# A hybrid decoder layer on one core: queries and keys copied out of PSUM once, head 0's keys split in a spare pad, two blocks of the final sums placed where block B11 was

## The chip, the cores and the metric

The kernel runs on one core of a Trainium2 chip. The core has five engines with an instruction queue each: TensorE (PE) multiplies matrices into eight banks of PSUM, VectorE (DVE), ScalarE (ACT) and GpSimd (POOL) compute on SBUF, DVE and ACT also on PSUM, and SyncE (SP) starts DMA transfers. The metric is the device time of one execution in microseconds. Before the change three runs took 1165.88, 1164.83 and 1165.71 us, a median of 1165.71.

## The reference

One layer of a decoder trunk in float32: 1024 tokens, 1024 channels, 8 heads of 64.

```
h = rms_norm(x, norm1_g)
q, k, v, glu_a, glu_b = split(h @ w_in)              # 512 columns each
q, k = rms_norm(q per head), rms_norm(k per head)
attn: z = q k / 8, strictly causal; weights[t,s] = sigmoid(z[t,s]) * prod_{s<j<t} (1 - sigmoid(z[t,j]))
c = glu_a * sigmoid(glu_b); causal depthwise conv of width 31; silu(layer_norm(c))
x = x + concat([attn, c]) @ w_out
h = rms_norm(x, norm2_g)
gate, val = split(h @ w_up)                          # 2816 columns each
x = x + (silu(causal_depthwise_conv3(gate)) * val) @ w_down
```

## The kernel before, in words

**Products.** Every float32 operand is split into a high and a low part of the type fp32r, and a product is three matrix multiplications: high by high (L281), low by high (L282) and high by low (L283). PE carries them all.

**Stages.** The kernel runs through these stretches of the profiled span: the input norm and its transposes (0 to 25 us); the projections of the glu, the conv, v, k and q of heads 0 to 3 (called v0, k0, q0), v of heads 4 to 7, and queries and keys of heads 4 to 7 together (qk0 to qk7, one for each tile of 128 tokens) up to some 240 us; attention, heads 0 to 7 one after the other, up to 457 us; the attention half of the output projection (opa), the second norm and its transposes up to 522 us; the up projection up to 939 us; and the down projection.

**Attention.** For a head, its keys are split into high and low on POOL (L905, L908), transposed on PE (kT, L922) and copied back; its queries are doubled by a DMA, transposed (qT, L956) and split by ACT and DVE. Then the queries go in eight tiles (tb 0 to 7) of 128 tokens, each against all keys up to its own: scores z on PE (L993, L996, with a mask L995), a sigmoid of −z into a row called nb and one of z into a row called wt (ACT, L1005 and L1008), a running product along nb (the scan on DVE, L1023), nb times wt on POOL (L1026), transposes of wt on PE (wT, L1049), their split (rest, L1053 on ACT or DVE, and tl, L1059 on DVE), and the product with v (po, L1065 and L1066). In the tile names the first number is the head and the next the tile: z0_4_1 is head 0, tile 4, second 512 columns. Where one head's tiles leave PE free, products of other stages fill in: qk0 to qk3, then the conv half of the output projection (op).

**What sets the order.** Up to the end of the second norm the order on PE, ACT, DVE and POOL is fixed by a planner in the kernel (class `Plan`). Every step has a cost, a due time ("key"), steps that it follows, and tokens of what it occupies: "s", "z" and "o" are PSUM banks, "nb" the four rows for the sigmoids, which are first the padded tiles ("pad") of the conv. The planner takes the step with the earliest start, or, among those within PATIENCE ns of it, the one with the earliest key, and writes the instructions in that order; `in_order` pins it. QK_TO and CONV_TO bound the keys over which the fillers are spread, W_SHIFT shifts the loads of the output weights, LEAD_LOAD says how far ahead of their use weights are loaded. From the up projection on, the framework's scheduler sets the order, and tile pools decide when a buffer is free.

**Norms of queries and keys.** `project` (k0, q0) and the steps for qk4 to qk7 leave the products in an "o" bank. ACT squares the eight groups of 64 columns with a sum each (L483, L804), POOL makes the reciprocal roots (`rstd`, L273), and ACT scales eight times into SBUF (L487, L808). The bank is held until then.

**Up and down projection.** The up projection multiplies by Strassen's scheme in blocks: tiles called 11, 21, 22, S1 and so on of the normed input, with block B11 in the tile "hh0" of the pool hp. The down projection adds its products from PSUM into four blocks of sums, 11, 12, 21 and 22 (L1626 on DVE); each starts from x, loaded by SP (L1604). Blocks 11 and 21 lie in a pool `dn` that opens when hp is closed, 12 and 22 in buffers of the up projection.

Of the kernel before, what the change touches and what calls it, by code (L numbers as in the profile page):

```python
# [16 lines left out]
P = 128  # L17
# [14 lines left out]
LEAD_LOAD, LEAD_W = 14.0, 11.0  # L32
# [144 lines left out]
def kernel(  # L177
# [54 lines left out]
    const([P, 24], F32, "pad")  # L232

    ident = const([P, P], F32, "ident")
    make_identity(nc, ident)
    ident_b = const([P, P], BF16, "ident_b")
    nc.vector.tensor_copy(ident_b, ident)
    ident_r = const([P, P], F32R, "ident_r")
    nc.vector.tensor_copy(ident_r, ident)
# [46 lines left out]
    small = ctx.enter_context(tc.tile_pool(name="small", bufs=1))  # L286
    mix_ctx = ExitStack()
    mixp = mix_ctx.enter_context(tc.tile_pool(name="mixp", bufs=1, reuse_waits="tile"))
    attn_out = mixp.tile([P, ND // 2, S], F32, tag="attn_out", name="attn_out")
# [4 lines left out]
    for tag in ("v0", "k0", "q0", "k1", "q1", "v1"):  # L294
        tile_of = qkvp.tile([P, 2, D], F32, tag=tag, name=f"x_{tag}")
        if tag not in ("v0", "k0"):
            xs.append(tile_of)
# [3 lines left out]
    wp = in_ctx.enter_context(tc.tile_pool(name="wp", bufs=1, side="right", reuse_waits="tile"))  # L301
    hp = hp_ctx.enter_context(tc.tile_pool(name="hp", bufs=1, side="right", reuse_waits="tile"))
# [33 lines left out]
    for n in range(2):  # L336
        h_hi.append(hp.tile([P, ND, HS], F32R, tag=f"hh{n}", name=f"h_hi{n}"))
        h_lo.append(hp.tile([P, ND, HS], F32R, tag=f"hl{n}", name=f"h_lo{n}"))
# [9 lines left out]
                 "qd": 2, "squares": 1, "whl": 8, "pair": 2, "norm": 4, "xsum": 2, "cacc": 2, "term": 3, "ln": 4},  # L348
# [93 lines left out]

    def project(part, blk, ws, pairs, ats):

        done.setdefault((part, blk), [])
        for pair, at_ in zip(pairs, ats):
# [31 lines left out]
            def square(d=d, pair=pair, dst=dst, o=o):  # L478
                d["sq"], d["rs"] = [small.tile([P, 8], F32, tag=f"{tag}8_{o.index}", name=f"{tag}_{part}{blk}_{pair}") for tag in ("sq", "rs")]
                d["to"] = dst().rearrange("p t (h d) -> p (t h) d", d=DH)  # L480
                d["from"] = d["ps"].rearrange("p t (h d) -> p (t h) d", d=DH)
                for i in range(8):
                    nc.scalar.activation(d["to"][:, i, :], d["from"][:, i, :], AF.Square, accum_out=d["sq"][:, i:i + 1])  # L483

            def scale(d=d):
                for i in range(8):
                    nc.scalar.activation(d["to"][:, i, :], d["from"][:, i, :], AF.Copy, scale=d["rs"][:, i:i + 1])  # L487

            a = add("ACT", 3500, square, T(at_ + 6), [m])
            b = add("POOL", 2700, lambda d=d: rstd(d["rs"], d["sq"], 1.0 / DH), T(at_ + 6), [a])  # L490
            a = add("ACT", 1850, scale, T(at_ + 6), [b])
            o.users += [a]
            done[part, blk] += [a]
# [287 lines left out]
    def queries_keys_in(t, at_):  # L781
# [3 lines left out]
        for k in range(ND):  # L785
            def products(k=k):
                if k == 0:
                    d["ps"] = bank(o, [P, 512], f"qk{t}")
                for part in "qk":
                    if (part, 1) not in qkv:  # L790
                        qkv[part, 1] = qkvp.tile([P, NT, 256], F32, tag=f"{part}1", name=f"{part}1")
# [8 lines left out]
        def square():  # L800
            d["sq"], d["rs"] = [small.tile([P, 8], F32, tag=f"{tag}8_{o.index}", name=f"{tag}_qk{t}") for tag in ("sq", "rs")]
            d["to"] = [qkv["qk"[i // 4], 1][:, t, i % 4 * DH:(i % 4 + 1) * DH] for i in range(8)]
# [301 lines left out]
    def w_out_rows(k):  # L1104
        room = plan.token("whl")

        def load():
            if not wd:
                for part in ("hh0", "hl0"):
                    wd[part] = hp.tile([P, 4 * S], F32R, tag=part, name=f"w_{part}")  # L1110
# [553 lines left out]
```

## Time and profile before

| what | value |
|---|---|
| median of three runs | 1165.71 us |
| profiled execution, its own time | 1162.9 us |
| its span | 1161.1 us |
| mean granted clock of TensorE | 0.987 |
| instructions | 16180 |
| transfers | 116.50 MB, 100 GB/s on average |

The page's span runs from the first to the last recorded instruction; the execution's own time is 1.8 us longer. In the windows, a row gives the window, its length, and then for each engine the busy time and, in brackets, the number of instructions: PE, its weight loads, DVE, ACT, POOL; after them the granted clock (1.00 is full speed), the share in which DMA engines were busy, and GB/s. In the table of waits a row gives the engine and line that waited, the engine, tile and line that released it, and the total, the number and the longest of the waits. In the timeline a row gives start, duration, engine, line, operation, output and input, and in square brackets the idle time before it with its releaser. Matmuls are pipelined, so their durations overlap; what one costs is the distance of the starts.

### The profile page before, as it was taken

How to read it: one execution, taken by the hardware profiler on the slowest of the kernel's cores; microseconds unless marked ns; L12 is line 12 of the kernel's file. 1: busy time of each engine (PE TensorE's matmuls, PEld its weight loads, DVE VectorE, ACT ScalarE, POOL GpSimd, SP SyncE). 2: the span in 40 equal slices, each digit the busy share in tenths (PEclk: the TensorE clock that was granted, in tenths of full speed). 3: DMA queues.
4: the chain of work that ended last, by engine and by line, in shares of the span. 5: the costliest groups of instructions: out<-in, count | busy, mean ns of one | idle time of the engine just before them, and what ended most of it. 6: DMA issues, size and time to landing. Idle time of an engine off the chain costs nothing.

```text
span 1161.1 us, 16180 instructions
## 1 busy us (share of the span) xinstructions
PE 1118.5 (96%) x5734; PEld 936.9 (81%) x5734; DVE 909.5 (78%) x1199; ACT 640.3 (55%) x1335; POOL 603.2 (52%) x505
## 2 busy tenths in 40 slices
PE   6999999989999997979999999999999989999998
PEld 5888899767788886868888888888888867888886
DVE  5399995549998888889887777777677679887895
ACT  6255576586987885554434333434333466766680
POOL 6077965486666652545522332233313167877880
PEclk8999999999999998989999999999999999999999
DMA  8011103122743114432332222222222461134303
GB/s 276 19 56 55 55 2 91 47 102 95 232 126 110 55 39 153 154 127 65 118 109 71 93 73 91 73 91 73 91 86 79 133 247 70 77 145 146 130 16 145
DMA packets 108638, 116.50 MB, mean 100 GB/s; under 512 B 20782, under 2 KB 88590, under 8 KB 108558
## 3 DMA queue, kind: packets, MB, share of 16 engines
q1 hardware_dynamic: 108414, 114.95, 30.0%
q8 instruction: 45, 0.74, 0.3%
q10 hardware_dynamic: 144, 0.52, 0.1%
q14 instruction: 35, 0.29, 0.1%
HBM read 82.95 MB, written 28.31 MB: 96 GB/s over the span
## 4 chain that ended last, share of the span: by engine, by line
PE 84%; DVE 6%; POOL 4%; ACT 3%; issue 2%; DMA 1%; SPq 0%; POOLq 0%; DVEq 0%; ACTq 0%
PE dn L1623 16%; PE u_S L281 7%; PE u_S L282 7%; PE u_S L283 7%; PE u L282 5%; PE u L281 5%; PE u L283 5%; PE wT L1049 2%; POOL attn_out L602 2%; PE po L1066 2%; PE v L281 1%; PE po L1065 1%; PE v L282 1%; PE v L283 1%; PE z L996 1%
## 5 line engine op out<-in xcount | busy, mean ns | idle before, releaser
L1623 PE MATMUL dn<-wd,wd 128*128 128x512 f32 x924 | 212.4, 390 | 5.3 <-DVE c L1626 2.7
L1623 PEld LDWEIGHTS dn<-wd,wd 128*128 128x128 f32 x924 | 172.6, 188 | 44.9 <-DVE c L1626 4.8
L1626 DVE TENSOR_TENSOR c<-dn,c 128x512 f32<-128x512 f32 x144 | 95.2, 683 | 24.1 <-PE dn L1623 22.8
L602 POOL TENSOR_TENSOR attn_out<-attn_out 128x512 f32<-128x512 f32 x60 | 83.3, 1389 | 54.2 <-ACT attn_out L599 50.4
L1532 ACT CAST wd<-rawd 128x512 fp32r<-128x512 f32 x154 | 87.0, 618 | 42.1 <-PE dn L1623 15.8
L1026 POOL TENSOR_TENSOR wt<-wt,nb 128x128 f32<-128x128 f32 (+3 forms) x64 | 78.2, 1228 | 56.6 <-DVE nb L1023 34.1
L282 PE MATMUL u_S<-bT,aS 128*128 128x512 f32 x264 | 102.7, 389 | 0.0
L283 PE MATMUL u_S<-bT,aS 128*128 128x512 f32 x264 | 102.7, 389 | 0.0
L281 PE MATMUL u_S<-bT,aS 128*128 128x512 f32 x264 | 102.4, 389 | 0.0
L277 ACT CAST aS<-rawu 128x512 fp32r<-128x512 f32 x63 | 39.0, 621 | 94.8 <-PE u_S L283 70.6
L1023 DVE TENSOR_TENSOR_SCAN nb<-nb,one 128x128 f32<-128x128 f32 (+3 forms) x64 | 85.3, 1344 | 6.8 <-ACT nb L1005 6.6
L1533 DVE TENSOR_TENSOR wd<-whole,wd 128x512 fp32r<-128x512 f32 x110 | 73.7, 683 | 10.7 <-ACT wd L1532 8.4
L1392 POOL TENSOR_TENSOR s<-rawu 128x512 f32<-128x512 f32 x21 | 29.9, 1426 | 99.5 <-DMA rawu<-in_w_up_dram 89.3
L1531 ACT COPY whole<-rawd 128x512 f32<-128x512 f32 x110 | 63.0, 584 | 29.7 <-DMA rawd<-in_w_down_dram 15.7
L1398 POOL TENSOR_TENSOR rawu<-rawu 128x512 f32<-128x512 f32 x21 | 29.0, 1381 | 82.3 <-DVE a L278 82.3
L282 PE MATMUL u<-b,a 128*128 128x512 f32 x176 | 70.0, 398 | 0.0
L281 PE MATMUL u<-b,a 128*128 128x512 f32 x176 | 69.9, 397 | 0.0
L283 PE MATMUL u<-b,a 128*128 128x512 f32 x176 | 69.2, 393 | 0.0
L277 ACT CAST a<-rawu 128x512 fp32r<-128x512 f32 x63 | 39.0, 621 | 51.5 <-PE u_S L283 34.7
L1487 DVE SCALAR_TENSOR_TENSOR y<-gv,cols_a,y 128x1023 f32<-128x1023 f32 (+1 forms) x44 | 58.6, 1333 | 8.3 <-ACT y L1485 8.2
L1533 POOL TENSOR_TENSOR wd<-rawd,wd 128x512 fp32r<-128x512 f32 x44 | 57.5, 1324 | 11.6 <-ACT wd L1532 9.7
L278 DVE TENSOR_TENSOR a<-rawu,a 128x512 fp32r<-128x512 f32 x63 | 47.0, 748 | 15.8 <-ACT a L277 15.8
(286 smaller groups left out, 3363.7 us busy)
## 6 DMA issues: line engine op xcount, KB each, us to landing
rawu<-in_w_up_dram SPq DMA_DIRECT2D x44, 512.0 KB
act_d<-y SPq DMA_DIRECT2D x22, 512.0 KB
rawd<-act_d SPq DMA_DIRECT2D x22, 512.0 KB
rawd<-in_w_down_dram SPq DMA_DIRECT2D x22, 512.0 KB
rawo<-in_w_out_dram SPq DMA_DIRECT2D x8, 512.0 KB
m<-conv_d SPq DMA_DIRECT2D x16, 256.0 KB
xt<-in_x_dram SPq DMA_DIRECT2D x8, 512.0 KB
x_part<-xt SPq DMA_DIRECT2D x8, 512.0 KB
```

What stands on the lines that cost most here:

```text
L277: nc.scalar.copy(hi, src)
L281: nc.tensor.matmul(ps, a_hi, b_hi, start=first, stop=False)
L282: nc.tensor.matmul(ps, a_hi, b_lo, start=False, stop=False)
L283: nc.tensor.matmul(ps, a_lo, b_hi, start=False, stop=last)
L602: last = add("POOL", 1310, lambda e=e: nc.gpsimd.tensor_tensor(d["c"], d["c"], e["t"], op=ALU.add), key(m, 16), [x, last])
L1023: nc.vector.tensor_tensor_scan(rev, rev, one.to_broadcast([P, w]), 1.0, op0=ALU.mult, op1=ALU.bypass)
L1026: nc.gpsimd.tensor_tensor(d["wt"][:, :w], d["wt"][:, :w], d["nb"][:, o + 1:S + 1], op=ALU.mult)
L1531: nc.scalar.copy(whole, src)
L1532: nc.scalar.copy(t[:, 0], src)
L1533: lo_engine.tensor_tensor(t[:, 1], whole, f32(t[:, 0]), op=ALU.subtract)
L1623: nc.tensor.matmul(ps, a[:, tok], b, start=first and m == 0, stop=last and m == 2, skip_group_check=True)
L1626: nc.vector.tensor_tensor(sums[c][s], ps, sums[c][s], op=ALU.add)
```

## The change

Six things, all in one edit (lines with "after" are those of the changed kernel):

1. `normalized()` (L447 to L470 after): one copy of the bank into SBUF, by ACT or DVE as the planner finds, and the "o" token is given back behind it. The squares are then taken from SBUF, all eight into one small tile `junk`, the scales in place. k0, q0 and qk4 to qk7 use it, twelve in all. For that, q and k of heads 4 to 7 become one tile, qk1.
2. Head 0's keys are split into a spare conv pad (`first_keys`, an "nb" token) instead of the tile "keys", which lies where the second half of the normed input was; so the split does not wait for the last use of that input (`second_used`), but the transposes and copies behind it do. The split's key is EARLY = 4 before the head instead of 2.6.
3. The first tile of the normed input, h_hi[0], later a part of the output weights and then block B11, lies in a pool of its own, hp0, that lives until the end. Sums 11 and 21 of the down projection are one tile c_1 in its place.
4. Constants: LEAD_LOAD 14 to 17, PATIENCE 50 to 200, QK_TO 6 to 7, W_SHIFT 0 to 0.5.
5. The identity is built in attn_out and only its fp32r copy is kept.
6. The constant pad shrinks from 24 to 8 columns.

The diff, cut to its core:

```diff
-LEAD_LOAD, LEAD_W = 14.0, 11.0
+LEAD_LOAD, LEAD_W = 17.0, 11.0
-HORIZON, PATIENCE = 3.0, 50
+HORIZON, PATIENCE = 3.0, 200
-QK_FROM, QK_TO = -3.0, 6.0
+QK_FROM, QK_TO = -3.0, 7.0
+EARLY = 4.0
-W_SHIFT = 0.0
+W_SHIFT = 0.5
...
+    made = attn_out[:, 1, :P]
+    make_identity(nc, made)
...
+    ident = f32(ident_r)
...
+    junk = const([P, DH], F32, "junk")
...
+    hp0 = in_ctx.enter_context(tc.tile_pool(name="hp0", bufs=1, side="right", reuse_waits="tile"))
...
-        h_hi.append(hp.tile([P, ND, HS], F32R, tag=f"hh{n}", name=f"h_hi{n}"))
+        h_hi.append((hp if n else hp0).tile([P, ND, HS], F32R, tag=f"hh{n}", name=f"h_hi{n}"))
...
+    def normalized(name, d, o, m, to, at_):
+        r = plan.token("rs8")
+        def out_of(eng):
+            (nc.scalar.copy if eng == "ACT" else nc.vector.tensor_copy)(to(), ...)
+        def square():
+            d["sq"], d["rs"] = [small.tile([P, 8], F32, tag=f"{tag}8_{r.index}", name=f"{tag}_{name}") for tag in ("sq", "rs")]
+            for i in range(8):
+                nc.scalar.activation(junk, to()[:, i * DH:(i + 1) * DH], AF.Square, accum_out=d["sq"][:, i:i + 1])
+        def scale():
+            for i in range(8):
+                group = to()[:, i * DH:(i + 1) * DH]
+                nc.scalar.activation(group, group, AF.Copy, scale=d["rs"][:, i:i + 1])
+        c = add({"ACT": 600, "DVE": 690}, out_of, T(at_), [m])
+        o.users += [c]
+        a = add("ACT", 3500, square, T(at_), [c], [r])
+        b = add("POOL", 2700, lambda: rstd(d["rs"], d["sq"], 1.0 / DH), T(at_), [a])
+        a = add("ACT", 1850, scale, T(at_), [b])
+        r.users += [a]
+        return a
...
     def unit(h):
         blk = h // 4
-        ready = list(qk_done.values()) if blk else done["k", 0] + second_used
-        kst, khl = plan.token("kst"), plan.token("khl")
+        ready = list(qk_done.values()) if blk else done["k", 0]
+        kst, khl = plan.token("kst"), plan.token("khl") if h else plan.token("nb", free=True)
...
+                nbs[khl.index] = None
+                stage["k"] = cp.tile([P, KC - 1 + S], F32R, tag=f"pad{khl.index}", name="first_keys")[:, :S]
...
-        k2 = split_op("k", lambda: big["keys"][:, :S], 0, base - 2.6, ready, khl)
+        k2 = split_op("k", staged, 0, base - (2.6 if h else EARLY), ready, khl)
...
-            a = add("PE", 300, turn, base - 2.5, k2, [s])
+            a = add("PE", 300, turn, base - 2.5, k2 + second_used, [s])
...
+    sums = hp0.tile([P, 4, D], F32, tag="hh0", name="c_1")
+    sums = {c: [sums[:, 2 * i + k // 2, k % 2 * HS:(k % 2 + 1) * HS] for k in range(4)] for i, c in enumerate(("11", "21"))}
...
-    sums = {c: quarters([dn.tile([P, D], F32, tag=f"c{c}_{k}", name=f"c{c}_{k}") for k in range(2)]) for c in ("11", "21")}
```

What it moves. First PE where attention begins, before. Of each group of rows the first is shown: qk7 and qk1 are queries and keys of heads 4 to 7 for tiles 7 and 1, kT0 and qT0 the transposes of head 0's keys and queries, lnT1 transposes of the conv's norm.

```order
L281 MATMUL qk7_2483<-hi_qk_3_2171,h_hi1_172 128x512
L281 MATMUL qk1_2561<-hi_qk_0_2069,h_hi0_170 128x512 [waits Activation_49]
L922 MATMUL kT0_0_2599<-ident_r_111,keys_2554 128x128 [waits DVE_49,Pool_49]
L922 MATMUL kT0_1_2604<-ident_r_111,keys_2554 128x128 [waits PE_49,Activation_49]
L664 MATMUL lnT1_2_2610<-ident_104,attn_out_130 128x128 [waits DVE_49]
L664 MATMUL lnT1_3_2630<-ident_104,attn_out_130 128x128 [waits Activation_49]
L993 MATMUL z0_0_0_2635<-keys_2554 128x256
L993 MATMUL z0_1_0_2639<-keys_2554 128x256
```

The same place on PE after the change:

```order
L287 MATMUL qk7_2460<-hi_qk_3_2196,h_hi1_174 128x512
L939 MATMUL kT0_0_2527<-ident_r_117,first_keys_1944 128x128 [waits DVE_49,PE_49]
L939 MATMUL kT0_1_2535<-ident_r_117,first_keys_1944 128x128 [waits DVE_49,PE_49]
L973 MATMUL qT0_0_2540<-ident_r_117,attn_out_110 128x128 [waits DMAHW2_49,DMAHW3_49,DVE_49,PE_49]
L678 MATMUL lnT1_0_2554<-ident_r_117,attn_out_110 128x128 [waits Activation_49]
L287 MATMUL qk1_2560<-hi_qk_0_2106,h_hi0_172 128x512 [waits DVE_49]
L973 MATMUL qT0_1_2575<-ident_r_117,attn_out_110 128x128 [waits DMAHW7_49,DMAHW4_49,Activation_49]
L1010 MATMUL z0_0_0_2585<-keys_2548 128x256 [waits Activation_49]
L1010 MATMUL z0_1_0_2592<-keys_2548 128x256
```

The key transposes now follow the last product of qk7 directly, and the conv's and the queries' transposes come behind them; before, fifteen of qk1's products stood ahead of them (and qT0 and two of lnT1 among the products of qk7 and qk1), and they waited for POOL.

Second, ACT's sigmoids into the rows of head 0, before, with the row's name nb0_... as output and the score's as input:

```order
L1005 ACTIVATE nb0_0_2646<-z0_0_0_2635 128x128 [waits DMAHW3_49,DVE_49,PE_49]
L1005 ACTIVATE nb0_1_2653<-z0_1_0_2639 128x256 [waits DMAHW4_49,PE_49]
L1005 ACTIVATE nb0_0_2646<-z0_2_0_2663 128x384 [waits PE_49,Pool_49]
L1005 ACTIVATE nb0_1_2653<-z0_3_0_2669 128x512 [waits PE_49,Pool_49]
L1005 ACTIVATE nb0_4_2733<-z0_4_0_2699 128x512 [waits DMAHW2_49,DMAHW0_49]
L1005 ACTIVATE nb0_1_2653<-z0_5_0_2744 128x512 [waits PE_49]
L1005 ACTIVATE nb0_6_2803<-z0_6_0_2794 128x512 [waits DMAHW4_49,DMAHW7_49,DVE_49,PE_49]
L1005 ACTIVATE nb0_7_2837<-z0_7_0_2828 128x512 [waits DMAHW3_49,PE_49,Activation_49]
```

And after:

```order
L1022 ACTIVATE nb0_0_2596<-z0_0_0_2585 128x128 [waits DMAHW0_49,PE_49]
L1022 ACTIVATE nb0_1_2607<-z0_1_0_2592 128x256 [waits PE_49]
L1022 ACTIVATE nb0_0_2596<-z0_2_0_2611 128x384 [waits DVE_49,PE_49]
L1022 ACTIVATE nb0_1_2607<-z0_3_0_2624 128x512 [waits PE_49]
L1022 ACTIVATE nb0_0_2596<-z0_4_0_2688 128x512 [waits PE_49,Pool_49]
L1022 ACTIVATE nb0_1_2607<-z0_5_0_2728 128x512 [waits DVE_49,PE_49]
L1022 ACTIVATE nb0_0_2596<-z0_6_0_2753 128x512 [waits PE_49,Pool_49]
L1022 ACTIVATE nb0_1_2607<-z0_7_0_2776 128x512 [waits Pool_49]
L1022 ACTIVATE nb1_0_2888<-z1_0_0_2876 128x128 [waits DMAHW1_49,PE_49]
```

Before, tiles 4, 6 and 7 of head 0 had rows of their own; now rows nb0_0 and nb0_1 take turns through the whole head, and the other two come in with head 1.

Third, PE at the end of attention, before. op7 is the last tile of the conv half of the output projection, wT7 and po7 belong to head 7; of each group the first row is shown.

```order
L993 MATMUL z7_6_1_4865<-keys_2554 128x384 [waits PE_49,Activation_49]
L281 MATMUL op7_1_4830<-w_hh0_3137,m7_4508 128x512
L993 MATMUL z7_7_0_4878<-keys_2554 128x512 [waits Activation_49]
L1065 MATMUL po7_0_4798<-rest_2555 128x256
L993 MATMUL z7_7_1_4894<-keys_2554 128x512 [waits PE_49,Activation_49]
L1049 MATMUL wT7_2_0_4902<-ident_104,wt7_4_4766 128x128 [waits Pool_49]
L1065 MATMUL po7_2_4901<-rest_2555 128x256 [waits DVE_49,Activation_49]
L1049 MATMUL wT7_3_0_4942<-ident_104,wt7_6_4858 128x128 [waits PE_49,Pool_49]
L1049 MATMUL wT7_3_1_4948<-ident_104,wt7_6_4858 128x128 [waits PE_49]
L1065 MATMUL po7_2_4901<-rest_2555 128x256 [waits Activation_49]
```

And after:

```order
L1010 MATMUL z7_6_1_4847<-keys_2548 128x384 [waits PE_49,Activation_49]
L1082 MATMUL po7_0_4807<-rest_2533 128x256 [waits DVE_49]
L287 MATMUL op7_0_4799<-w_hh0_3217,m7_4509 128x512
L1010 MATMUL z7_7_0_4869<-keys_2548 128x512 [waits Activation_49]
L1082 MATMUL po7_0_4807<-rest_2533 128x256
L1010 MATMUL z7_7_1_4880<-keys_2548 128x512 [waits PE_49,Activation_49]
L1066 MATMUL wT7_2_0_4890<-ident_r_117,wt7_4_4770 128x128 [waits Pool_49]
L287 MATMUL op7_1_4911<-w_hh0_3217,m7_4509 128x512 [waits Activation_49]
L1082 MATMUL po7_2_4889<-rest_2533 128x256 [waits DVE_49]
L287 MATMUL op7_1_4911<-w_hh0_3217,m7_4509 128x512
L1066 MATMUL wT7_3_0_4943<-ident_r_117,wt7_6_4857 128x128 [waits PE_49,Pool_49]
L1066 MATMUL wT7_3_1_4948<-ident_r_117,wt7_6_4857 128x128 [waits PE_49]
```

Before, three products of op7 were left behind z7_6_1; now there are eighteen, six ahead of z7_7_0, three behind the transposes wT7_2, and the rest among the products po7_2 and the transposes wT7_3.

In the down projection SP now issues the eight loads of c_1 ahead of the load rawd7; before, the loads of sums 11 and 21 stood behind it.

More of the change, by code (lines that the diff above doesn't have):

```diff
@@ L293 @@
     xs = []
-    for tag in ("v0", "k0", "q0", "k1", "q1", "v1"):
-        tile_of = qkvp.tile([P, 2, D], F32, tag=tag, name=f"x_{tag}")
+    for tag, n in (("v0", 1), ("k0", 1), ("q0", 1), ("qk1", 2), ("v1", 1)):
+        tile_of = qkvp.tile([P, n, 2, D], F32, tag=tag, name=f"x_{tag}")
         if tag not in ("v0", "k0"):
-            xs.append(tile_of)
+            xs += [tile_of[:, i] for i in range(n)]
     conv_ctx = ExitStack()
@@ L476, in project @@
                 continue
[L478 to L493, printed above, removed]
+            done[part, blk].append(normalized(f"{part}{blk}_{pair}", d, o, m, lambda dst=dst: dst().rearrange("p t c -> p (t c)"), at_ + 6))
     HALF = (KC - 1) // 2
@@ L788, in products @@
                     d["ps"] = bank(o, [P, 512], f"qk{t}")
-                for part in "qk":
-                    if (part, 1) not in qkv:
-                        qkv[part, 1] = qkvp.tile([P, NT, 256], F32, tag=f"{part}1", name=f"{part}1")
+                if "both" not in qkv:
+                    qkv["both"] = both = qkvp.tile([P, NT, 512], F32, tag="qk1", name="qk1")
+                    qkv["q", 1], qkv["k", 1] = both[:, :, :256], both[:, :, 256:]
                 hi, lo = [w_qk[k // 2][part].rearrange("p k b c -> p k (b c)") for part in ("hi", "lo")]
@@ L798, in queries_keys_in, with to @@
         second_used.append(m)
[L800 to L814 removed]
+        def to():
+            return qkv["both"][:, t, :]
+        qk_done[t] = normalized(f"qk{t}", d, o, m, to, at_ + 6)
     for t in range(4, NT):
@@ L855, in square @@
         def square():
-            d["sq"], d["rs"] = [small.tile([P, 8], F32, tag=f"{tag}8_{o.index}", name=f"{tag}_qk{t}") for tag in ("sq", "rs")]
+            d["sq"], d["rs"] = [small.tile([P, 8], F32, tag=f"{tag}8_{room.index}_", name=f"{tag}_qk{t}") for tag in ("sq", "rs")]
             d["squares"] = squares(room, f"squares{t}")
@@ L897, in high @@
             def high(eng):
-                if not big:
-                    big["keys"], big["rest"] = [hp.tile([P, 4 * S], F32R, tag=tag, name=name) for tag, name in (("hh1", "keys"), ("hl1", "rest"))]
                 d["t"] = dst().rearrange("p (t a d) -> p t a d", a=2, d=DH)
@@ L918, in turn @@
             def turn(i=i, d=d, s=s):
-                keys = big["keys"]
+                keys = stage["k"]
                 d["pt"] = bank(s, [P, 512], f"kT{h}_{i}", F32R)
@@ L933, in unit @@
         vst = plan.token("vst")
[L934 removed]
+        v2 = split_op("v", lambda: part_of(kept("rest"), vst.index, S), h % 2, base - 1.5, k2 + done["v", blk] + second_used, vst)
         if not blk:
@@ L1108, in load @@
             if not wd:
-                for part in ("hh0", "hl0"):
-                    wd[part] = hp.tile([P, 4 * S], F32R, tag=part, name=f"w_{part}")
+                for part, pool in (("hh0", hp0), ("hl0", hp)):
+                    wd[part] = pool.tile([P, 4 * S], F32R, tag=part, name=f"w_{part}")
             w_conv[k] = part_of(wd["hh0"], k, D), part_of(wd["hl0"], k, D)
```

54 lines of the change are left out of this document (26 added, 28 removed).

## The prediction

> **What bounds the kernel now.** I read the page's table of engines first, then the busy time by stage, then the matrix engine's waits, and last the timeline at the places that the change touches.
>
> ```profile
> PE 1118.5 (96%) x5734; PEld 936.9 (81%) x5734; DVE 909.5 (78%) x1199; ACT 640.3 (55%) x1335; POOL 603.2 (52%) x505
> ```
>
> The matrix engine (PE) is busy 1118.5 of 1161.1 us. The change takes no product away, so all it can win lies in the 42.6 us in which PE stands, and in stretches with a lower clock. The windows by stage say where those are; the first column after the window is its length, then busy time of PE, weight loads, DVE, ACT and POOL, the granted clock, and the transfers.
>
> ```profile
> 0.00:25.00 25.00, 15.76 (x89) 11.91 (x90) 13.11 (x17) 17.70 (x29) 15.19 (x22) 0.86 0.84 283
> 140.00:240.00 100.00, 97.06 (x700) 89.94 (x699) 66.97 (x93) 62.74 (x298) 57.70 (x61) 1.00 0.18 57
> 240.00:300.00 60.00, 52.89 (x319) 42.58 (x317) 45.12 (x57) 47.94 (x123) 43.12 (x45) 0.97 0.37 117
> 437.00:457.00 20.00, 14.07 (x79) 11.66 (x78) 17.83 (x17) 11.42 (x21) 6.55 (x4) 0.83 0.47 163
> 480.00:522.00 42.00, 36.10 (x155) 28.39 (x154) 36.49 (x48) 25.89 (x49) 23.68 (x23) 0.88 0.42 138
> 522.00:939.00 417.00, 417.00 (x1841) 344.45 (x1840) 315.56 (x383) 162.20 (x235) 140.34 (x97) 1.00 0.28 90
> 939.00:975.00 36.00, 30.71 (x125) 22.30 (x124) 33.88 (x54) 22.75 (x43) 26.37 (x20) 1.00 0.44 161
> ```
>
> PE stands 9.2 us at the start and 5.9 in the second norm (480 to 522); the change leaves both stages' work as it is. It stands 2.9 us in the projections with norms (140 to 240), 7.1 at the start of attention (240 to 300), 5.9 at its end (437 to 457) and 5.3 where the down projection begins (939 to 975): **21.2 us in four places** are within the change's reach. The up projection has no gap. The waits of PE name the releaser (total us, times, longest):
>
> ```profile
> PE z L993 <- ACT wt L1008: 5.6, 5, 2.9
> PE po L1066 <- DVE tl L1059: 2.8, 2, 2.5
> PE dn L1623 <- DVE c L1626: 2.7, 4, 1.6
> PE dn L1623 <- DVE gv L1626: 1.5, 2, 0.8
> PE po L1065 <- ACT m L1267: 1.5, 1, 1.5
> PE qk L281 <- ACT k L808: 1.0, 1, 1.0
> PE v L281 <- DVE v L472: 0.8, 1, 0.8
> PE kT L922 <- POOL rest L908: 0.6, 1, 0.6
> PE k L281 <- ACT k L487: 0.4, 1, 0.4
> ```
>
> **The change part by part. (A) One copy out of PSUM.** Today a bank with queries or keys is held through eight squares, the reciprocal root on POOL and eight scales on ACT. The change frees it after one copy.
>
> ```profile
> 212.57 0.22 ACT L804 ACTIVATE q<-qk 128x64 f32<-128x64 f32 x1 [6.01 <-PE qk L283]
> 212.69 0.19 ACT L804 ACTIVATION_READ_ACCUMULATOR q<-qk 128x1 f32 x1
> 212.78 0.22 ACT L804 ACTIVATE q<-qk 128x64 f32<-128x64 f32 x1
> 199.26 0.59 ACT L472 COPY v<-v 128x512 f32<-128x512 f32 x1 [4.91 <-PE v L283]
> 186.70 0.69 DVE L472 COPY v<-v 128x512 f32<-128x512 f32 x1 [3.58 <-PE v L283]
> ```
>
> Price: twelve copies of the same shape as v's, five on ACT (0.59) and seven on DVE (0.69): 3.0 us and 4.8 us. In 140 to 240 ACT is free for 37 us and DVE for 33, so the copies lie beside PE. The new squares all write one tile, `junk`, and each waits for ACT's one before; now a square and its reading follow at 0.20 us (212.57 to 212.78) though they last 0.22 and 0.19. Without overlap a pair takes at most 0.41, so a group of eight costs between nothing and 8 x 0.21 = 1.7 us more, twelve groups up to 20 us of ACT. In 140 to 240 even that fits in 37 us; only the last group (qk7), which now stands among attention's first sigmoids, can matter, and it is counted in B. What ends is the three waits k, v and qk: 0.4 + 0.8 + 1.0 = 2.2 us, if nothing else is late there; the ends are 0 (another wait takes their place) and 2.9 (all of the stretch's idle time). **I take −2.0.**
>
> [...]
>
> **(B) The start of attention.** Head 0's keys are split on POOL into a spare pad, so the split no longer waits for the last product that uses the second half's activations, and stands earlier in POOL's order.
>
> ```profile
> 242.48 0.63 POOL L905 TENSOR_SCALAR keys<-k 128x512 fp32r<-128x512 f32 x1 [0.15 <-PE qk L282]
> 243.19 1.79 POOL L908 TENSOR_TENSOR keys<-k,keys 128x512 fp32r<-128x512 f32 x1
> 246.93 0.91 PE L922 MATMUL kT<-ident_r,keys 128*128 128x128 f32 x8 [0.55 <-POOL rest L908]
> 249.19 0.36 PE L993 MATMUL z<-keys 128*128 128x256 f32 x1
> 260.25 0.51 PE L993 MATMUL z<-keys 128*128 128x512 f32 x1 [2.95 <-ACT wt L1008]
> 260.00:280.00 20.00, 18.13 (x107) 15.02 (x107) 18.79 (x26) 13.79 (x32) 13.94 (x15) 0.91 0.20 66
> 271.94 0.28 PE L993 MATMUL z<-keys 128*128 128x256 f32 x1
> ```
>
> The split's 0.63 + 1.79 us leave the chain from 242.48 to 246.93, so the transposes can follow the products of qk7 at once: fifteen products of 0.23 us, some small transposes and 0.55 us of wait stand between now, so 4 to 5 us earlier on PE, and 2 us or more for the first scores, since kT's copies and the queries' split still lie between. PE's total doesn't fall by that: the products of qk1, which filled the time, now come behind. What is won is the waits, if the first rows of the head run ahead of the need. Against it: head 0 has two rows now instead of four or five (the order in the section on the change); one row's turn is a sigmoid, a scan and a product, and four tiles share each. The rows by size:
>
> ```profile
> L1023 DVE TENSOR_TENSOR_SCAN nb<-nb,one 128x1024 f32<-128x1024 f32 x8 | 18.2, 2280 | 0.1
> L1026 POOL TENSOR_TENSOR wt<-wt,nb 128x1024 f32<-128x1024 f32 x8 | 16.0, 2002 | 10.0 <-DVE nb L1023 6.9 <-ACT wt L1008 1.7 <-ACT rest L1053 1.5
> L1005 ACT ACTIVATE nb<-z 128x512 f32<-128x512 f32 x48 | 29.0, 607 | 3.2 <-PE z L996 3.0
> ```
>
> The longest tile holds its row for 2 x 0.61 + 2.28 + 2.00 = 5.5 us. Taking scan, product and sigmoid as proportional to length (256, 512, 768 and 1024 columns on the second row), that row is bound for 5.5 x 2.5 = 13.8 us of head 0, which lasts 22.75 us now (249.19 to 271.94). So there are 9 us of room for a dozen hand-overs, 0.75 us each. They fit barely: each can wait behind one other instruction of ACT (0.6 us, as v's copy above). Ends: all idle time of the stretch and its lost clock go, 7.1 + 1.8 (20 us at 0.91) = −8.9; or the rows bind, +8 (priced among the rivals). Nearer to the middle: earlier start worth 2, shared rows and slower squares taking a little back. **I take −1.5.**
>
> **(C) The end of attention.** PE waits there for scans, casts and copies with nothing left to fill in. PATIENCE, QK_TO and W_SHIFT change the planner's order: behind the score z7_6_1 now stand 18 filler products of the out-projection instead of 3.
>
> ```profile
> 438.39 0.39 PE L283 MATMUL op<-w_hh,m 128*128 128x512 f32 x1
> 438.62 0.39 PE L993 MATMUL z<-keys 128*128 128x512 f32 x1
> 448.61 1.05 ACT L1197 CAST hio<-rawo 128x1024 fp32r<-128x1024 f32 x1
> ```
>
> One product takes 0.23 us of PE (438.39 to 438.62), so the 15 moved ones fill 3.5 us of the 5.9. The cast m, which held PE for 1.5 us, now stands behind the last transposes' casts, too. The clock of 0.83 means 3.4 of 20 us lost; if the gaps shrink, part of that returns, +1 of gain. Against it, two casts of the out-projection's weights (1.05 us each) have moved behind the attention's last casts, and the first attention half of that projection waits for them; I let 1 to 2 us of them show. −3.5 − 1 + 2 = **−2.5**, ends 0 and −5.9.
>
> **(D) The start of the down projection.** Sums 11 and 21 are loaded when B11's last product is done, in the last block pair of the up projection, instead of when a pool opens behind it.
>
> ```profile
> 939.77 3.88 SPq L1604 DMA_DIRECT2D c<-x_d  x8
> 944.29 1.37 DVE L1626 TENSOR_TENSOR c<-dn,c 128x512 f32<-128x512 f32 x2 [1.05 <-DMA c<-x_d]
> 945.04 1.66 PE L1623 MATMUL dn<-wd,wd 128*128 128x512 f32 x6 [1.59 <-DVE c L1626]
> ```
>
> DVE stands 1.05 us for those loads and PE 1.59 us behind DVE. Eight loads at 0.48 us of issue (3.88 / 8) move ahead of rawd7's load on SP, which then waits 3.9 us longer for its turn; its products come only behind eighteen others on PE. With the loads early, DVE starts at 943.24 and the wait falls to 0.5 or so. But DVE is busy 33.9 of 36 us here, so the later waits of 0.7 to 0.8 us stay. **I take −1.0**, ends 0 and −4.2 (2.7 + 1.5, all waits for sums).
>
> **(E)** The identity built elsewhere and the smaller pad cost nothing: their work lies in the first 25 us, beside the load of x (transfers at 0.84). Without that cover it would be one copy of 128 x 128. LEAD_LOAD starts weight loads earlier in a stretch with transfers at 0.18. The rest of the second plan moves a few instructions on DVE and ACT; ±1, taken as 0.
>
> Sum: −2.0 − 1.5 − 2.5 − 1.0 = **−7.0 us**. The profiled execution took 1162.9 us (a span of 1161.1 and 1.8 around it), 2.8 below the median of 1165.7; it would become 1155.9, and the median **1158.7 us**.
>
> **Rivals.** *The two rows bind (slower side).* If a tile of head 0 waits for its row at each of the four pairs as z did once for 2.95 us, that is 11.8 us of waits in place of 5.6: +6.2, and with another 1.8 us of lost clock +8.0. With A, C and D as above the sum is +2.5: 1168.2. It decides from 7.8 us on in B. For it: 0.75 us of slack a hand-over, and ACT busy 18.55 of 20 us there:
>
> ```profile
> 240.00:260.00 20.00, 16.47 (x92) 12.34 (x90) 8.20 (x11) 18.55 (x59) 17.59 (x20) 1.00 0.24 76
> ```
>
> Against it: even in the old order tiles 0 to 3 and 5 of head 0 shared two rows, and that cost one long wait. [...]
>
> *The stalls only change places.* Fillers spent at the end are missing at the start; A's waits go, D's too, B and C give nothing together: −3.0, 1162.7. For it: the amount of filler is fixed. Against it: early stalls are short of ACT, not of fillers.
>
> *The start is cleared.* Earlier keys let rows run ahead; B reaches −7: 1153.2. For it: 4 to 5 us of earlier transposes. Against it: ACT.
>
> **How the numbers follow.** Likeliest sum 0.48; rows bind 0.18; stalls change places 0.18; start cleared 0.16. A change under 0.2% (2.3 us) can't be told from none: below 1163.4 is faster, above 1168.0 slower. Faster: 0.48 + 0.16, and 0.08 of the third (its centre lies 0.7 inside): 0.72. Slower: 0.13 of the second. The rest, 0.15, is the same. The range runs from 1151.5 (start cleared and the tail's ends) to 1168.5 (rows bind); the likeliest case by itself spans 1155 to 1162.
>
> **What would show it.** A: no wait of qk, v or k for ACT or DVE in 140 to 240, PE busy above 99. B: kT before 243, z1's first score less than 24 us behind z0's, less idle time than 7 us in 240 to 300. C: PE busy above 16.5 of the last 20 us of attention and a clock over 0.83. D: no wait of DVE for c; PE's first wait under 0.6. I am wrong if head 0 takes 26 us or more, if the squares' pitch nears 0.41 and ACT holds PE in the projections, or if the moved casts hold the out-projection for more than 3 us.

## The result and the profile after

| kernel | median, us | ratio to before (95% interval) |
|---|---|---|
| before | 1165.27 | |
| changed | 1172.45 (1171.37 to 1174.97) | 1.0065 [1.0047, 1.0083] |

(The kernel before has a fourth run here, so its median is 1165.27 instead of 1165.71.) The change makes the kernel **7 us slower**, 0.65%. The forecast was 1158.7 us, 7 us faster, with a range up to 1168.5. The profiled execution took 1171.37 us, with a span of 1169.6. The first lines of its page:

```profile
span 1169.6 us, 16171 instructions
PE 1123.7 (96%) x5734; PEld 938.8 (80%) x5734; DVE 918.1 (78%) x1208; ACT 654.9 (56%) x1330; POOL 612.4 (52%) x512
```

The same 5734 instructions of PE, ACT 14.6 us busier, the span 8.5 us longer. The windows by stage (length; busy PE, weight loads, DVE, ACT, POOL; clock; transfers) put the loss in two places. The borders are those of before up to 437 us and lie later behind it, with the stages; the row of before for 300 to 437, which the prediction left out, was 135.03 us of PE at a clock of 1.00.

```profile
140.00:240.00 100.00, 98.39 (x716) 92.39 (x715) 66.15 (x96) 80.07 (x307) 63.79 (x66) 1.00 0.17 54
240.00:300.00 60.00, 51.28 (x310) 41.43 (x309) 46.39 (x58) 47.62 (x118) 38.30 (x38) 0.94 0.29 94
300.00:437.00 137.00, 133.58 (x871) 112.46 (x869) 123.51 (x146) 107.05 (x223) 88.75 (x78) 0.99 0.37 111
437.00:459.00 22.00, 18.18 (x115) 15.01 (x114) 19.83 (x21) 13.88 (x26) 10.03 (x7) 1.00 0.36 118
459.00:482.00 23.00, 22.36 (x99) 17.99 (x98) 14.70 (x22) 9.90 (x17) 6.10 (x9) 0.93 0.56 176
482.00:530.00 48.00, 37.83 (x166) 29.73 (x165) 38.31 (x50) 25.49 (x48) 23.87 (x24) 0.89 0.40 137
947.00:983.00 36.00, 31.20 (x127) 22.82 (x126) 35.52 (x56) 24.90 (x45) 28.28 (x22) 1.00 0.30 103
```

In the projections PE stands 1.6 us instead of 2.9, and at attention's end 3.8 instead of 5.9, at a clock of 1.00 instead of 0.83: both the way that was forecast, and both smaller than the terms A and C, 1.3 us for 2.0 and 2.1 us of filled gaps for 3.5. At attention's start it stands 8.7 instead of 7.1, at a clock of 0.94 instead of 0.97, and in the middle 3.4 instead of 2.0. In the second norm, 482 to 530, it stands **10.2 us** instead of 5.9. The waits of PE name that last one (total, times, longest):

```profile
PE h2T L1328 <- DVE h L1320: 9.7, 4, 4.9
PE wT L1066 <- issue: 4.1, 2, 3.2
PE dn L1642 <- DVE c L1645: 3.7, 3, 2.1
PE op L287 <- ACT prod L1177: 2.0, 1, 2.0
PE z L1010 <- ACT wt L1025: 1.9, 4, 0.8
PE v L288 <- DVE lo_v L437: 1.5, 1, 1.5
PE kT L939 <- POOL keys L925: 1.3, 1, 1.3
```

The waits for k, v's copy and qk are gone. In the same stretch another has come, 1.5 us at 182 us: the first products of v for heads 4 to 7 wait for lo_v, the low part of their weights, which DVE makes. The wait for h, 5.9 us before, is 9.7; wT waits 4.1 us in two pieces that the table of before does not have.

Three marks on PE's timeline split the loss. The first attention product of the output projection (opa) starts at 458.87 (456.56 before), the first product of the down projection at 946.97 (939.20 before), and the span ends 222.6 us behind that (221.9 before). So attention hands over 2.3 us later, the stretch of opa, second norm and up projection is 5.5 us longer, and the down projection 0.7. The two theories that follow from it: **the planner's new order in the second plan** costs the 5.5 us, or that stretch is late because attention hands over late and with the clock low (0.93 in 459 to 482 us; 1.00 in 457 to 480 before); and in attention, **ACT's queue**, not the shared rows, eats what the copies and the early keys win. A fourth mark says how much is eaten: head 0's first score starts at 241.84 (249.19 before), head 1's at 272.67 (271.94 before). Head 0 takes 30.8 us instead of 22.75, and the 7.4 us of its earlier start are gone before it ends.

### The profile page after: what moved, and what is told of

Its sections match the earlier page's. It is cut to its first block, busy times and chain, and to the rows that moved or that the text cites. A ratio compares the mean times of both kernels' runs of the same rounds, so it can differ in the third digit from the quotient of the medians.

```text
span 1169.6 us, 16171 instructions
## 1 busy us (share of the span) xinstructions
PE 1123.7 (96%) x5734; PEld 938.8 (80%) x5734; DVE 918.1 (78%) x1208; ACT 654.9 (56%) x1330; POOL 612.4 (52%) x512
## 4 chain that ended last, share of the span: by engine, by line
PE 70%; DVE 11%; ACT 7%; POOL 6%; DMA 3%; issue 3%; SPq 0%; ACTq 0%; DVEq 0%; POOLq 0%
PE dn L1642 8%; PE u_S L287 7%; PE u_S L289 7%; PE u_S L288 7%; PE u L288 5%; PE u L289 5%; PE u L287 5%; PE wT L1066 2%; DVE conv_a L589 2%; DMA rawd<-act_d 2%; ACT wd L1549 2%; PE v L288 1%; POOL attn_out L616 1%; PE v L289 1%; PE v L287 1%
## 5 line engine op out<-in xcount | busy, mean ns | idle before, releaser
L1076 DVE TENSOR_TENSOR tl<-wT,rest 128x512 fp32r<-128x512 f32 x80 | 53.3, 683 | 8.5 <-ACT rest L1070 7.4
```

## Experiments on the second plan

The second plan starts from nothing behind the first, and of all constants that changed only PATIENCE is read in it. So its order can be exchanged without touching the first plan's, and the other way about. The ratios of all experiments are to the kernel before, which ran beside each of them with medians of 1164.5 to 1165.5 us. The changed kernel was measured once, in four runs; a difference between two versions that were not measured side by side is uncertain by about 1 us more than their intervals say.

**E1, old order in the second plan.** Edit of the changed kernel:

```diff
-    def run(self, busy):
+    def run(self, busy, patience=PATIENCE):
+        self.patience = patience
...
-                rank = (max(start - PATIENCE, at[e]), op.key) ...
+                rank = (max(start - self.patience, at[e]), op.key) ...
...
-    plan.run({})          # the second plan
+    plan.run({}, 50)
```

> The changed kernel with PATIENCE 200 in the first plan and 50 in the second, which gives the order of opa, second norm and first up products back as it was. Theory (the second plan's order, changed by PATIENCE, costs what lies between the first opa product and the first dn product: 482.6 us before, 488.1 after, so 5.5 us): about 1167, the last wait for h of 4.9 us falls to about 2. Rival (that stretch is late because attention's end hands it over late, with the weight casts moved and the clock low): no change, about 1172.

Measured: 1167.38 us, 1.0024 [1.0013, 1.0034], as the theory has it. The waits for h fall from 9.7 to 5.9 us.

**E2, new order in the second plan of the kernel before**: the same edit there, with `plan.run({}, 200)`.

> The kernel before with PATIENCE 200 in the second plan alone; the order there is that of the changed kernel, attention is untouched. Theory (second plan's order): about 1170.5, 5 us slower than before, with the long wait for h. Rival (attention's end hands over late): no change, 1165.5.

Measured: 1171.53 us, 1.0058 [1.0043, 1.0073]. The order of the second plan alone makes the kernel before 6.8 us slower, and undoing it alone gives the changed kernel 5 us back. The four waits for h in E2 sum up to 9.7 us, as in the changed kernel. The rival, a late hand-over, is out: in E2 attention is untouched.

**Where in that order.** DVE ahead of the last transposes of the second norm, first in the changed kernel, then in E1 (bT are splits of the Strassen sums, h the second norm's products):

```profile
516.99 3.45 DVE L1341 TENSOR_TENSOR bT<-t,bT 128x512 fp32r<-128x512 f32 x2
520.35 1.74 DVE L1341 TENSOR_TENSOR bT<-raws,bT 128x512 fp32r<-128x512 f32 x1
522.02 1.40 DVE L1320 SCALAR_TENSOR_TENSOR h<-x,rs,g 128x512 f32<-128x512 f32 x2
```

```profile
514.39 3.46 DVE L1342 TENSOR_TENSOR bT<-t,bT 128x512 fp32r<-128x512 f32 x2
517.77 0.73 DVE L1321 SCALAR_TENSOR_TENSOR h<-x,rs,g 128x512 f32<-128x512 f32 x1
518.43 1.09 DVE L1342 TENSOR_TENSOR bT<-raws,bT 128x512 fp32r<-128x512 f32 x1
519.45 0.73 DVE L1321 SCALAR_TENSOR_TENSOR h<-x,rs,g 128x512 f32<-128x512 f32 x1
```

With 50 ns of patience the first half of h goes ahead of the last bT, since it can start earlier; with 200 ns both count as equal, the earlier key decides, and h queues behind a split of 1.7 us. The changed kernel's PE then stands 4.88 us, E1's 2.06 and 1.05:

```profile
522.90 1.94 PE L1328 MATMUL h2T<-ident_r,h 128*128 128x128 f32 x8 [4.88 <-DVE h L1320]
```

```profile
518.65 0.63 PE L1329 MATMUL h2T<-ident_r,h 128*128 128x128 f32 x4 [2.06 <-DVE h L1321]
520.33 0.63 PE L1329 MATMUL h2T<-ident_r,h 128*128 128x128 f32 x4 [1.05 <-DVE h L1321]
```

**E13, h ahead of the splits, with PATIENCE 200 kept.** Edit of the changed kernel, in the second norm's step for h:

```diff
-                ... op0=ALU.mult, op1=ALU.mult), key + 0.5, [f] + g2_ready)
+                ... op0=ALU.mult, op1=ALU.mult), key - 0.6, [f] + g2_ready)
```

> The changed kernel, with one edit: in the second plan the second norm's products h (DVE) have a key 1.1 earlier, so that with PATIENCE 200 they stand ahead of the splits bT of the tile before instead of behind them. Theory (the 5 us of the second plan's new order are h queued on DVE behind bT splits that wait for ACT; PE waits 4.9 us for the last h): that wait falls under 2.5 us, time 1166 to 1168, as with the plan's old order. Rival (other rows of the new order cost it): 1171 to 1173, no change.

Measured: 1169.19 us, 1.0034 [1.0022, 1.0045]: between the two, 3.3 us of the 5. The wait for h is gone altogether; others have come in its place, the two longest of which are these:

```profile
PE opa L287 <- DVE x L1302: 3.7, 2, 3.0
PE u L288 <- POOL b L1341: 3.1, 1, 3.1
```

It misses the theory's range by 1.2 us and the rival's by 1.8. So the queue of h on DVE is the larger part of the loss, as far as an edit can tell that puts other waits in its place. DVE has the same instructions to do; what PE waits for follows their order (9.7 us for h in the changed kernel, none here). What makes up the remaining 2 us of the order was not taken apart further.

## Experiments on the copies and squares

**E5, the squares' outputs apart.** The eight squares of a group write eight slices instead of one tile, so none waits for another; the planned order is the same on every engine.

```diff
-    junk = const([P, DH], F32, "junk")
+    junk = qkvp.tile([P, 8, DH], F32, tag="junk", name="junk")
...
-                nc.scalar.activation(junk, to()[:, i * DH:(i + 1) * DH], AF.Square, accum_out=...)
+                nc.scalar.activation(junk[:, i, :], to()[:, i * DH:(i + 1) * DH], AF.Square, accum_out=...)
```

> The changed kernel, with one edit: the eight squares of a group write eight slices of a tile instead of one shared tile, so that none waits for the one before. The planned order is the same on every engine. In the changed kernel the pitch of the dependent squares is 0.38 us (a group of 2.9 us), before it was 0.20 (1.6 us). Theory (ACT's queue at 240 to 260 us sets the start of attention: the conv norm's transposes hold the three s banks until ACT has read them, and the transposes wT0 wait for those banks, 1.0 and 3.2 us): pitch 0.20, the waits of wT0 fall by 1.4 to 2.8 us, time 1.5 to 3 us less, about 1170. Rival (those waits come from POOL's late products or the two rows): pitch 0.20 but no change beyond 0.7 us, about 1172.

Measured: 1169.96 us, 1.0038 [1.0025, 1.0051], some 2.5 us less than the changed kernel. The time is the one that the theory gave, but the waits of wT0 fall by 0.9 us only, less than its 1.4 to 2.8; where the rest comes from is said below.

**E7, E1 and E5 together.**

> The changed kernel with both edits: PATIENCE 50 in the second plan and the squares' outputs apart. If the two losses are independent (about 5 us and 1.5 to 3 us): 1164.5 to 1166, level with the kernel before. If the second plan's order alone matters: 1167.4 as with that edit alone.

Measured: 1164.01 us, 0.9987 [0.9978, 0.9996]: **the first version that beats both kernels**, by 0.13%, and 0.5 us below the range for two independent losses. Next to E1 the squares cost 3.4 us. The dependent squares, from the changed kernel's timeline of ACT, and the independent ones of E7:

```profile
245.21 0.28 ACT L457 ACTIVATE junk<-qk 128x64 f32<-128x64 f32 x1
245.35 0.22 ACT L457 ACTIVATION_READ_ACCUMULATOR junk<-qk 128x1 f32 x1
245.61 0.26 ACT L457 ACTIVATE junk<-qk 128x64 f32<-128x64 f32 x1
```

```profile
244.18 0.28 ACT L458 ACTIVATE junk<-qk 128x64 f32<-128x64 f32 x1
244.33 0.23 ACT L458 ACTIVATION_READ_ACCUMULATOR junk<-qk 128x1 f32 x1
244.42 0.28 ACT L458 ACTIVATE junk<-qk 128x64 f32<-128x64 f32 x1
```

The pitch is 0.24 us with outputs apart, and 0.38 to 0.40 us with the shared output; before the change, with the squares taken from PSUM, it was 0.20. In the changed kernel the next instruction follows the group of qk7 at 248.15, 2.9 us behind its start, in E7 at 246.09, 1.9 us behind it (1.6 us for a group before). So of the 1.3 us that a group grew, 1.0 is the shared output, and 0.3 stays with outputs apart.

**What the squares hold up.** In the changed kernel the transposes wT0 wait 0.94 and 3.16 us for something that the profile names only "issue". The order shows what they wait for besides the products on POOL: a bank of the kind "s". There are three, and the conv norm's transposes lnT sit in them until ACT has read them twice, last with the line conv_out:

```profile
249.33 0.76 ACT L705 ACTIVATE conv_out<-lnT,cols_a 128x512 f32<-128x512 f32 x1
254.78 0.79 ACT L705 ACTIVATE conv_out<-lnT,cols_a 128x512 f32<-128x512 f32 x1
```

```profile
250.19 0.30 PE L1066 MATMUL wT<-ident_r,wt 128*128 128x128 f32 x1 [0.94 <-issue]
255.66 0.66 PE L1066 MATMUL wT<-ident_r,wt 128*128 128x128 f32 x2 [3.16 <-issue]
```

249.33 + 0.76 and 254.78 + 0.79 are 250.09 and 255.57, each 0.1 us ahead of the transposes. In E7 the first of these two waits is gone; the second stands, again 0.1 us behind the end of conv_out (253.54, wT at 253.64). In the queue ahead of those lines stand the squares of qk7 (2.9 us), its scales (2.0 us) and the scores' sigmoids. That the bank is what the transposes wait for is read from these times; no run gives the planner another bank.

The other part of the squares' cost lies ahead of attention. In the four profiles with the shared output and this order of the first plan (the changed kernel, E1, E6, E13) PE waits 1.5 or 1.6 us for lo_v at v of heads 4 to 7, and head 0's first score starts at 241.5 to 242.7 us. In the four with outputs apart (E5, E7, E14, E15) this wait is missing, PE has next to no gap in the projections, and the score starts at 239.8 to 241.0. The row of E7:

```profile
140.00:240.00 100.00, 99.91 (x728) 93.92 (x727) 66.47 (x98) 73.88 (x311) 67.29 (x68) 1.00 0.18 58
```

1.5 us for lo_v and 0.9 for wT0 are 2.4 us, close to the 2.5 that E5 gains. By which instructions ACT's longer squares delay lo_v was not followed.

**E9, the scales of qk4 to qk7 on DVE**, on top of E7; the first plan is ordered anew.

```diff
-        a = add("ACT", 1850, scale, T(at_), [b])
+        def scale_all():
+            group = to().rearrange("p (h d) -> p h d", d=DH)
+            nc.vector.tensor_tensor(group, group, d["rs"].unsqueeze(2).to_broadcast([P, 8, DH]), op=ALU.mult)
+        a = add("DVE", 750, scale_all, T(at_), [b]) if name.startswith("qk") else add("ACT", 1850, scale, T(at_), [b])
```

> The changed kernel with the second plan's old order and the squares apart (1164.0), and the scales of qk4 to qk7 as one instruction on DVE instead of eight on ACT (2.0 us of ACT a group); the planner orders the first plan anew. Theory (ACT's queue at the start of attention holds the s banks): the remaining wait of wT0_1 for 3.2 us goes or shrinks below 1, time 1159 to 1162.5. Rival (the order at that place is what costs, whoever scales): the waits move to other transposes, 1163.5 to 1166.

Measured: 1165.70 us, 1.0010 [0.9998, 1.0023]. The wait of wT0_1 is gone, and the time is not better: kT now waits 2.0 us for conv_out and op 2.3 us for DVE. The rival holds: its range has the time. Single stalls of this stretch can be moved, but not cashed in one by one.

**E10, head 0's keys split late again**, on top of E7 (token "khl", the tile "keys", second_used ahead of the split, key 2.6).

> The changed kernel with the second plan's old order and the squares apart (1164.0), and head 0's keys split as before: into the tile keys, behind the last use of the second half's input, key 2.6. If the early keys gain (prediction, 1.5 us) this is 1165 to 1167; if early keys only pile work on ACT while it is the bound (theory), it is 1161 to 1164. The first plan is ordered anew, so a few us more or less may be the order's.

Measured: 1167.53 us, 1.0022 [1.0011, 1.0033], 3.5 us slower than E7, just above what the early keys' gain would give. But the marks do not show that gain where the prediction put it. Head 0's first score starts 1.8 us later than in E7 (242.6 against 240.8), head 1's first score 1.8 us earlier (268.8 against 270.6), and the first opa product 3.3 us later (460.1 against 456.8). The loss comes behind head 0, in an order made anew. That the early keys gain by an earlier start is not shown. E10 also gives head 0 its other rows back (POOL sets up a third one for it at 256.1, in E7 none before head 1). Head 0 is shorter with them, 26.2 us against 29.8, but PE stands 8.2 us in 240 to 300 against 7.8 in E7: more rows do not lessen its idle time there.

## Experiments on the sums and the constants

**E6, the sums 11 and 21 back in their old pool**, hp0 undone.

> The changed kernel with the sums 11 and 21 back in a pool that opens behind the up projection; the two plans are untouched. Theory (the early sums only move DVE's backlog: dn runs 42 products without a wait instead of 18 and then waits 2.1 us for DVE): no change, within 0.7 us of the changed kernel. Rival (the prediction's: the early loads are worth 1 us): 1 us slower than the changed kernel. Third (the changed order costs): 1 us faster.

Measured: 1172.62 us, 1.0065 [1.0052, 1.0079]: no difference that shows, though with intervals of 1.5 to 2 us a loss of 1 us could hide in it. The profiles agree: from the first product of the down projection to the end are 222.8 us here and 222.6 in the changed kernel. In the changed kernel PE runs 42 products of the down projection without a wait, where it was 18, and then waits for DVE, which is held by the last activation's product y:

```profile
946.97 10.21 PE L1642 MATMUL dn<-wd,wd 128*128 128x512 f32 x42
959.30 0.96 PE L1642 MATMUL dn<-wd,wd 128*128 128x512 f32 x3 [2.12 <-DVE c L1645]
```

```profile
955.49 0.67 DVE L1645 TENSOR_TENSOR c<-dn,c 128x512 f32<-128x512 f32 x1
956.09 1.96 DVE L1507 TENSOR_TENSOR y<-gv,y 128x1024 f32<-128x1024 f32 x1
957.97 0.68 DVE L1550 TENSOR_TENSOR wd<-whole,wd 128x512 fp32r<-128x512 f32 x1
```

DVE is busy 35.5 of the 36 us there. The early loads let PE run ahead into the same backlog.

**E8, all four constants as before**, with the new code.

> The changed kernel with all four constants as before (LEAD_LOAD 14, PATIENCE 50, QK_TO 6, W_SHIFT 0): the code's part of the change alone, with the second plan in its old order. Theory (earlier keys and an ACT queue with longer squares lose at the start of attention what the freed banks win, and the constants had been fitted to the new code): 1167 to 1175, slower than before. Rival (the loss is all in the constants): 1161 to 1165, faster than before or level.

Measured: 1166.29 us, 1.0010 [1.0001, 1.0019], between the two ranges: 6 us below the changed kernel and about 1 above the kernel before. So the code by itself wins nothing in the old order.

**E11, E8 with the squares apart.**

> The changed kernel with all constants as before and the squares apart. The squares cost 2.5 to 3.4 us where the constants are new; if ACT's queue is as much the bound in this order: 1163 to 1164.5, faster than the kernel before by 1 to 2 us. If they are covered here: 1166, as with the constants alone.

Measured: 1165.43 us, 1.0002 [0.9994, 1.0011], level with before: less than expected, 0.9 us from the squares instead of 2 to 3.

**E12, E11 with head 0's keys as before**: the copies, the early sums and the small things are left.

> All constants as before, the squares apart, head 0's keys as before: what is left of the change is the copy out of PSUM, the smaller things (identity, pad) and the early sums. Prediction's step A (the waits for k, v and qk go, 2.0 us): 1162.5 to 1164. Rival (the twelve copies and the order made anew take that back): 1165 to 1169.

Measured: 1166.85 us, 1.0012 [1.0004, 1.0021]. In its windows PE has no gap at all in the projections, and more than before at the start of attention, at a low clock:

```profile
140.00:240.00 100.00, 100.00 (x726) 94.11 (x725) 68.58 (x98) 73.39 (x320) 56.08 (x60) 1.00 0.16 47
240.00:300.00 60.00, 50.18 (x277) 40.45 (x277) 44.12 (x54) 42.66 (x99) 39.69 (x44) 0.86 0.35 118
```

Step A works to the letter and the time is lost again 50 us later: head 0's first score starts at 249.32, before the change at 249.19. It is not PE that it waited for: the transposes kT wait 2.7 us for POOL (rs_qk) and 0.7 for ACT. The time lies in the rival's range.

**E3, PATIENCE 50 in the first plan alone**, and **E4, the new constants in the code before.**

> The changed kernel with PATIENCE 50 in the first plan and 200 in the second. If PATIENCE also spoils attention's order (transposes wT0 placed ahead of the scores of tile 4, a stall of 3.3 us at 252 us, another stretch at low clock at 300 to 320): 4 to 6 us faster, about 1167. If the two rows of head 0 or ACT's queue are behind these stalls: no change beyond 1 us, about 1172.

> The kernel before with the four new constants alone (LEAD_LOAD 17, PATIENCE 200, QK_TO 7, W_SHIFT 0.5). Theory (orders changed by the constants carry the whole loss): 1170 to 1173. Rival (the two rows and the new squares carry the attention part of the loss, some 2 to 6 us, and constants only the second plan's 5): about 1168 if the end of attention gains what the changed kernel gains there.

Measured: E3 1180.99 us, 1.0133 [1.0107, 1.0159]; E4 1190.57 us, 1.0226 [1.0211, 1.0242]. Both lie outside what was expected, 9 and some 18 us to the slower side. In E4 attention hands over at 477.4, 21 us later than before. With the old code the new constants are ruinous in the first plan, with the new code (and the second plan left as it was) they gain, E7 against E11, some 1.5 us. In E3 one of them, PATIENCE, put back by itself in the first plan costs 8.5 us next to the changed kernel. Which of the four does it in E4 was not tried.

**E14 and E15, h ahead in other company.** E14 is E7 with E13's edit, E15 is E5 with it.

> PATIENCE 50 in the second plan, squares apart (1164.0), and the same earlier key for h. If h is what PE waits for there also in the old order (5.7 us in four waits): 1161.5 to 1163.5. If ACT or the splits become late instead: 1164 to 1166.

> The changed kernel with its own constants, the squares apart and h's key earlier. If the two repairs are independent (2.5 to 3.4 us and 5): 1162.5 to 1165, faster than the kernel before or level with it.

Measured: E14 1163.04 us, 0.9983 [0.9974, 0.9992], the lowest median here and 9 us below the changed kernel, but not told apart from E7 by its interval; E15 1166.90 us, 1.0021 [1.0012, 1.0031]. In E14 the waits for h are gone, others of 1.0 to 1.6 us stand in their place, and from the first opa product to the first of the down projection are 480.3 us against 480.9 in E7. E15 misses its bounds: it is 3.1 us below E5, as E13 is 3.3 below the changed kernel, so the two repairs add up, but with PATIENCE 200 h's repair is short of the 5 us.

## Why the prediction was wrong

**E was the step that failed.** "The rest of the second plan moves a few instructions on DVE and ACT; ±1, taken as 0." It costs 5 us in the changed kernel (E1) and 6.8 in the one before (E2). What should have been asked of it is one question: which of DVE's instructions stands ahead of the one that PE already waits for? The table of waits named it, h with 5.9 us, and h had moved behind a split. The sum set the stage aside with the words that the change leaves its work as it is. Its work is the same; its order isn't.

**A was right about the place and wrong about the worth.** The three waits went and PE's idle time there fell from 2.9 to 1.6 us (busy above 99 of 100 was named as the sign, it is 98.4), in E7 to 0.1 and in E12 to 0; the 1.6 us are the new wait for lo_v, the case that the end 0 named (another wait takes their place). But E12 is not faster: there the next stage starts when ACT and POOL let it. A wait removed ahead of a stage that another engine starts was worth nothing here, and the term should have been 0 with −2.0 as its end, as far as E12's order, made anew, can say.

**The squares were the second step that failed: bounded rightly and priced wrongly.** The bound was 0 to 1.7 us a group; a group measured 2.9 us instead of 1.6, 1.3 us more, near the upper end. The sum took a little back for them, within B's −1.5. The chain through one output adds 0.13 us a pair (1.0 us for the eight of qk7, the changed kernel against E7), and 0.04 more stay with outputs apart (a pitch of 0.24 us, 0.20 before). "Even that fits in 37 us" is true of the sum and failed in the order: the wait for lo_v, 1.5 us at 182, comes with the shared output and goes with it. Nor does it hold behind 240, where ACT (the fourth of the busy times) has half a microsecond left. Together the squares cost 2.5 us (E5), 3.4 (E7 against E1) and 2.3 (E15 against E13); with the old constants, 0.9 (E11 against E8):

```profile
240.00:260.00 20.00, 14.72 (x76) 10.75 (x75) 9.41 (x13) 19.53 (x60) 14.05 (x17) 0.89 0.28 86
```

**B got its early start, and not its worth.** The key transposes start at 238.15, 8.8 us earlier, the first score at 241.84, 7.4 earlier, more than the 4 to 5 and the 2 forecast. But head 0 then takes 30.8 us, past the 26 that the prediction named as the sign of being wrong, and PE's idle time in 240 to 300 grows by 1.6 us instead of falling. Versions with late keys are slower by 3.5 us (E10 against E7) and 1.4 (E12 against E11), which looks like the 1.5 forecast; the orders there are made anew, and E10's marks put its loss elsewhere, so that the number is near may be luck. That head 0's two rows kept PE idle is not borne out: with more rows, in E10, PE stands as long. ACT's waits in 240 to 272 us of the changed kernel name no row:

```profile
ACT rest L1070 <- DVE tl L1076: 1.3, 1, 1.3
ACT gate L682 <- POOL conv_out L706: 0.2, 1, 0.2
ACT rest L1070 <- PE wT L1066: 0.2, 1, 0.2
```

The longest wait, as far as the times can say, was for the "s" banks behind ACT's queue, a case that no rival named. The rival reckoned with lost clock, and some is lost at this place: the granted clock is 1.00 from 240 to 254 us, 0.88 in 254 to 256, where the 3.16 us stall ends, and 0.50 from 256 to 262; over the window above it is 0.89.

**C was right in its own window.** The fillers fill, idle time falls by 2.1 us and the clock is at 1.00. PE is busy 16.2 of the last 20 us (439 to 459), a little under the 16.5 named as the sign. Of what is left 2.0 us are a filler's own wait, op for ACT's prod. The low clock has in part moved on: it is 0.93 in 459 to 482, and was 1.00 in 457 to 480 before. Behind the moved casts the out-projection waits 0.6 us (opa for m on DVE, which stands behind a split of the weights), not the 2 taken for them. And the fillers are missing earlier: between the last product of qk and the first of op lie 10.8 us (301.8 to 312.6) instead of 8.7, and 300 to 437 loses 1.4 us and some clock (0.99 for 1.00). "The stalls only change places" was the third case, and for attention as a whole it is close to what happened.

**D was wrong in the way it warned of.** DVE's wait for the loads is gone, its backlog isn't, and the sum of PE's waits for sums is 4.6 us against 4.2 before; PE's first wait is 2.1 us, where under 0.6 was to show that D works. The 1.0 us should have been 0, as far as E6 can tell.

Set together: the second plan's order, 5 us, and the squares, 2.3 to 3.4, make the changed kernel 7 us slower than it was; without these two it is 1.5 us faster (E7) where 7 were forecast.

## What to carry to other kernels

Where a planner's constant is changed for one stage, compare the order of every stage that reads it, and first of all the place of those instructions that the slowest engine already waits for. Outputs that nobody reads ordered the instructions that write them here (a square every 0.38 to 0.40 us into one place, every 0.24 into eight, in E7): give each its own place if the engine is busy. Before a wait is counted as won, ask whether the next stage waits for the engine that it frees: in E12 PE was busy 100.00 of 100 us in the projections, and head 0's first score came no earlier (249.32 us, before the change 249.19).

## What was not expected of the hardware

Twelve executions of E9, one program, lie between 1162.2 and 1168.7 us, those up to 1163.5 with a granted clock of 0.986 to 0.990 and those above 1167 with 0.980 to 0.984; before the change the runs beside it spread from 1162.95 to 1167.19 at 0.984 to 0.988. The clock is not all of it: executions of E13 at a granted clock of 0.985 lie between 1165.34 and 1170.51 us. So the time of one program here carries 4 to 7 us of chance, as much as the effects looked for, and only medians of ten or more runs told versions apart that differ by 0.15%.
